# A softmax over rows: eight neighbouring rows per partition, taken from one block of 1024 rows or from 128 long stretches

## The chip, the cores and the metric

The kernel runs on one core of a Trainium2 chip, with the other cores idle. The metric is the device time of one execution in microseconds (us). The verdicts call 2% a difference. A profile is one execution; its span is about 2 us shorter than the time. HBM is the chip's main memory. KB and KiB both stand for 1024 bytes here, MB for a million.

A ratio below is the mean time of one kernel's fast runs over that of the kernel before in the same rounds, so it is not quite the ratio of the medians that stand beside it.

## The reference

The input has 32 x 512 = 16384 rows of 1024 float32 numbers, 67.1 MB, and the output is as large.

```python
def reference(x, temperature):            # temperature = 0.5
    scaled = x / temperature
    shifted = scaled - np.max(scaled, axis=-1, keepdims=True)
    exp_x = np.exp(shifted)
    return (exp_x / np.sum(exp_x, axis=-1, keepdims=True)).astype(np.float32)
```

Every row is computed by itself, so it doesn't matter which row sits in which partition, as long as it is stored where it came from.

## The kernel before

There are 16 tiles of 128 partitions with 8 rows each, in six buffers. The SyncE queue issues the loads, the ScalarE queue the stores. A tile goes through VectorE (maximum of each row, for four rows at a time), ScalarE (exponential and sum) and VectorE again (division in place), and is stored as a whole. When a tile's store has been issued, the load that will reuse its buffer is recorded; SyncE then waits until that store has landed.

```python
TILES = [[8]] * 16
BUFS = 6
# ...
    def dram(t, i):
        k = sum(TILES[i])
        block = t[P * first[i] : P * (first[i] + k), :]
        return block.rearrange("(p k) d -> p k d", p=P, k=k)
# ...
    def load():
        i = len(tiles)
        if i < len(TILES):
            xt = data.tile([P, sum(TILES[i]), d], f32, name="xt")
            nc.sync.dma_start(out=xt, in_=dram(xf, i))
            tiles.append(xt)
# ...
    def store(g):
        i, _, _, part = groups[g]
        if part:
            a, k = part
            nc.scalar.dma_start(out=dram(of, i)[:, a : a + k, :], in_=tiles[i][:, a : a + k, :])
            if a + k == sum(TILES[i]):
                load()
```

## Time and profile before

| | before |
|---|---|
| time, median of 3 runs | 318.23 us (318.12 to 318.53) |
| profiled span | 316.0 us |
| VectorE, ScalarE busy | 75%, 47% |
| data moved | 134.25 MB, 425 GB/s over the span |
| packets of 32 KB | 2048 loads, 2048 stores |

The transfers bound this kernel: the prediction below shows the lines and how they say so. The rate of the transfers in 40 equal slices of the span, from the page of the kernel before:

```profile
GB/s 332 411 452 423 373 460 415 452 425 431 436 427 440 427 444 423 444 419 448 415 452 411 452 408 456 423 444 427 436 431 432 440 423 444 419 444 419 452 411 274
```

One slice is 7.9 us. Neighbouring slices swing by some 30 GB/s presumably because packets of 32 KB are counted as wholes; averaged over two slices the rate is near 433. The dip to 373 in the fifth slice is where the first store begins. The last slice holds the end of the last store.

In the kernel before a 32 KB packet takes 1213 ns almost without exception: 53 of the 2048 load packets take more than 1240 ns, none of the 2048 store packets does. 49 of the 53 are in two places, the very first packets of the kernel and the moments before the first store.

### The profile page before, as it was taken

Reading aid. Unit: us, or ns where it says so; the run is one execution under the profiler, and the core shown is the slowest. Engines: PE = TensorE matmul, PEld = TensorE weight load, DVE = VectorE, ACT = ScalarE, POOL = GpSimd, SP = SyncE. Lnnn points to the kernel's source line nnn. Section 1 sums busy time; section 2 is a strip of 40 time slices with the busy share of each in tenths; the row PEclk is TensorE's granted clock in tenths of the full one; section 3 lists DMA queues with packets and bytes.
Section 4 is the critical chain, followed back from the end, with each engine's and each line's share of the span. In section 5 each row is a group of like instructions: output and inputs, shape, how many; then the busy total and the mean of one; then the engine's idle time right before and its main releaser. Section 6 shows DMA issues by size and latency. Waiting matters only on the chain.

```text
span 316.0 us, 620 instructions
## 1 busy us (share of the span) xinstructions
DVE 235.5 (75%) x224; ACT 149.6 (47%) x257; POOL 0.2 (0%) x4
## 2 busy tenths in 40 slices
DVE  0399999999689494994949859497693976949720
ACT  0176666666526255361554605546064560645500
POOL 0000000000000000000000000000000000000000
DMA  8999999999999999999999999999999999999996
GB/s 332 411 452 423 373 460 415 452 425 431 436 427 440 427 444 423 444 419 448 415 452 411 452 408 456 423 444 427 436 431 432 440 423 444 419 444 419 452 411 274
DMA packets 4612, 134.25 MB, mean 425 GB/s; under 512 B 512, under 2 KB 512, under 8 KB 512
## 3 DMA queue, kind: packets, MB, share of 16 engines
q1 hardware_dynamic: 2304, 67.11, 49.7%
q10 hardware_dynamic: 2304, 67.11, 49.2%
q14 instruction: 4, 0.03, 0.0%
HBM read 67.11 MB, written 67.11 MB: 425 GB/s over the span
## 4 chain that ended last, share of the span: by engine, by line
DVE 49%; DMA 32%; another core or an unknown queue 9%; ACT 5%; issue 1%; DVEq 0%; SPq 0%
DVE top L70 29%; DMA xt<-in_x_dram 20%; DVE xt L93 18%; DMA out_dram<-xt 12%; ACT xt L79 5%; DVE recip L91 1%; DVE bias L73 1%; DVEq L147 0%; SPq L61 0%
## 5 line engine op out<-in xcount | busy, mean ns | idle before, releaser
L79 ACT ACTIVATE xt<-xt,bias 128x1024 f32<-128x1024 f32 x128 | 145.4, 1137 | 136.8 <-DVE recip L91 119.4
L70 DVE TENSOR_REDUCE top<-xt 128x4 f32<-128x4096 f32 x32 | 141.3, 4416 | 62.6 <-DMA xt<-in_x_dram 62.6
L93 DVE TENSOR_SCALAR xt<-xt,recip 128x1024 f32<-128x1024 f32 x128 | 87.7, 749 | 1.1
L79 ACT ACTIVATION_READ_ACCUMULATOR xt<-xt,bias 128x1 f32 x128 | 23.9, 187 | 0.0
L79 ACT ACT_TABLE_LOAD x1 | 1.3, 1283 | 13.0 <-DMA xt<-in_x_dram 13.0
L91 DVE RECIPROCAL recip<-sums 128x4 f32<-128x4 f32 x32 | 5.5, 171 | 2.1 <-ACT xt L79 2.1
L73 DVE TENSOR_SCALAR bias<-top 128x4 f32<-128x4 f32 x32 | 5.4, 170 | 1.1
L133 POOL MEMSET const-bfloat16-1.0<- 128x1 bf16 x1 | 0.1, 101 | 0.0
L133 POOL MEMSET const-uint8-127<- 128x1 uint8 x1 | 0.1, 101 | 0.0
L133 POOL MEMSET const-float32-0.0<- 128x1 f32 x1 | 0.1, 98 | 0.2 <-issue 0.2
L133 POOL MEMSET const-float32-1.0<- 128x1 f32 x1 | 0.1, 98 | 0.0
## 6 DMA issues: line engine op xcount, KB each, us to landing
xt<-in_x_dram SPq DMA_DIRECT2D x16, 4096.0 KB, 50.2
out_dram<-xt ACTq DMA_DIRECT2D x16, 4096.0 KB, 38.6
```

The costliest lines, as they stand in the source:

```text
L70: nc.vector.tensor_reduce(out=top, in_=tiles[i][:, a : a + k, :], axis=mybir.AxisListType.X, op=extreme)
L73: nc.vector.tensor_scalar_mul(bias, in0=top, scalar1=-scale)
L79: nc.scalar.activation(tiles[i][:, a + b, :], tiles[i][:, a + b, :], mybir.ActivationFunctionType.Exp, bias=bias[:, b : b + 1], scale=scal ...
L91: nc.vector.reciprocal(recip, sums)
L93: nc.vector.tensor_scalar_mul(tiles[i][:, a + b, :], in0=tiles[i][:, a + b, :], scalar1=recip[:, b : b + 1])
L133: nc = _bacc.Bacc("TRN2", target_bir_lowering=False, num_devices=1)
```

## The change

The intent: let partition p own one long stretch, rows 128p to 128p+127, for the whole kernel, and let a tile take the next eight rows of every stretch. The tile's form in the core's memory and the run of one partition (8 rows, 32 KB) stay as they are. The distance in HBM between one partition's run and the next, called the pitch below, grows from 32 KB to 512 KiB.

```diff
     def dram(t, i):
-        k = sum(TILES[i])
-        block = t[P * first[i] : P * (first[i] + k), :]
-        return block.rearrange("(p k) d -> p k d", p=P, k=k)
+
+        rows = t.rearrange("(p r) d -> p r d", p=P)
+        return rows[:, first[i] : first[i] + sum(TILES[i]), :]
```

## The prediction

> **What bounds the kernel now.** I read the page of the profile from the top. Its first three parts nearly settle the matter, so I give them first.
>
> ```profile
> span 316.0 us, 620 instructions
> DVE 235.5 (75%) x224; ACT 149.6 (47%) x257; POOL 0.2 (0%) x4
> ...
> DMA  8999999999999999999999999999999999999996
> ...
> DMA packets 4612, 134.25 MB, mean 425 GB/s; under 512 B 512, under 2 KB 512, under 8 KB 512
> ...
> q1 hardware_dynamic: 2304, 67.11, 49.7%
> q10 hardware_dynamic: 2304, 67.11, 49.2%
> ```
>
> No compute engine is full: VectorE works 75% of the span, ScalarE 47%. The DMA row is 9 in all but the first and the last of 40 slices, and the two queues together fill 98.9% of the 16 DMA engines' span. So the kernel is bound by its transfers, from the first microsecond to nearly the last. Of the 2304 packets of a queue, 256 are under 512 B (16 transfers times 16 engines: the completion writes). The other 2048 are 16 tiles times 128 partitions: one packet is one partition's eight rows, 8 x 4 KB = 32 KB. Its mean duration is 0.497 x 16 x 316.0 / 2048 = 1.227 us on the load queue and 0.492 x 16 x 316.0 / 2048 = 1.215 us on the store queue. That is about 27 GB/s for one engine, 428 to 432 for sixteen.
>
> Next, the busy time by stretches, to see whether the rate depends on the mix of loads and stores (columns: stretch, its length, DVE, ACT, POOL, clock, DMA share, GB/s).
>
> ```profile
> 0.00:12.90 12.90, 0.00 (x0) 0.00 (x0) 0.20 (x4) 1.00 0.90 366
> ...
> 76.00:120.00 44.00, 35.40 (x34) 21.79 (x39) 0.00 (x0) 1.00 1.00 433
> 120.00:165.00 45.00, 31.80 (x32) 22.77 (x40) 0.00 (x0) 1.00 1.00 433
> ...
> 300.00:316.00 16.00, 2.35 (x4) 0.00 (x0) 0.00 (x0) 1.00 0.80 344
> ```
>
> The middle runs flat at 433 GB/s. A rate as flat as this in every stretch looks like the engines' own ceiling, not like memory that answers late now and then.
>
> Third, the waits and the chain that ended last, to see what the compute side hides.
>
> ```profile
> DVE top L70 <- DMA xt<-in_x_dram: 62.6, 12, 13.0
> ...
> 263.25 4.43 DVE top L70
> 267.71 0.17 DVE bias L73
> 267.88 0.09 DVE recip L91
> 267.99 2.74 DVE xt L93 x4
> 270.73 4.34 DVE top L70
> 275.17 0.18 DVE recip L91
> 275.38 2.74 DVE xt L93 x4
> 278.12 4.47 another core or an unknown queue
> 282.62 4.43 DVE top L70
> ```
>
> VectorE is idle for 62.6 us in all before the maximum of a new tile, always for a load. In the chain a tile comes every 282.62 - 263.25 = 19.37 us; VectorE works for about 14.9 us of it and waits 4.47 us. The page puts 49% of the chain on VectorE, but that is how it followed the releases. The period is that of the transfers: 8.39 MB (4.19 loaded, 4.19 stored) in 19.37 us is 433 GB/s, the very rate of the stretches.
>
> **What the Trainium skill says.** Three places bear on this, all on its page "DMA: Bandwidth & Descriptors".
>
> Section "Where 436 GB/s comes from" puts the ceiling of the 16 ports at 435.2 GB/s. The trace agrees: 433 in the steady part. Hence almost nothing can be gained by any layout: 435.2 / 433 is 0.5%.
>
> Section "Latency and other measured facts" has a row on HBM row pitch at large powers of two. It gives copies of tiles of 128 partitions x 16 KiB between HBM tensors, per direction: a pitch of 512 KiB between partitions gave 207 GB/s, 2 MiB 164, 4 MiB and 8 MiB 103, and 4 MiB padded by 4 KiB gave 214, called full. The page says that the cause (aliasing of HBM channels) is inferred, not verified. Twice 214 is 428, close to the 425 of this page; the trace of before shows nothing of a larger pitch.
>
> Section "The descriptor swizzle" says which partitions an engine serves: four neighbours and four more 32 further on. So at one moment sixteen engines work on partitions four apart. If they run in step, their addresses in HBM are 4 x 32 KB = 128 KiB apart now, and will be 4 x 512 KB = 2 MiB apart. The page of before doesn't list partitions by engine; no run here shows it.
>
> **The change part by part.** Nothing on an engine changes. Compared in the built programs, both kernels have the same rows in the same order on all engines: 130 on VectorE, 35 on ScalarE, 3 on SyncE. The SBUF side is the same too: 128 partitions with 32 KB each. What changes is only the address of each partition's 32 KB in HBM, for loads and stores alike. Before, tile i is one block of 4 MB, and partition p starts 32 KB after p-1. Afterwards partition p owns rows 128p to 128p+127, and tile i takes rows 8i to 8i+7 of each; partition p starts 128 x 4 KB = 512 KB after p-1.
>
> Added or removed instructions: 0. Softmax works row by row, so no result depends on which row sits in which partition. Packets: the run is 8 adjacent rows, still 32 KB contiguous, so still 2048 per direction and the same 134.2 MB. Issue: the pattern is partition, then one run, as before; the 32 transfers are issued long ahead of or under other transfers, and cost nothing now. Ends of the kernel: every transfer still uses all partitions, so the first load and the last store keep their form.
>
> What is left is the duration of a packet, and here I chose the skill's row for 512 KiB: it is exactly the new pitch, in both directions, as here. Estimate from it: 214 / 207 = 1.034 times the packet time of before.
> - Transfers in the span now: (0.497 + 0.492) x 316.0 = 312.5 us. The other 3.5 us are the first issue and the gaps at the end.
> - Afterwards, with the whole effect: 312.5 x 1.034 = 323.1 us, plus 3.5 = 326.6 us of span, plus the 318.23 - 316.0 = 2.2 us by which the time exceeds the profiled span: 328.8 us, 3.3% slower.
> - With no effect: 318.2.
>
> Nothing hides it. The transfers are the path throughout, and VectorE's wait of 4.47 us per tile grows by the same 19.37 x 0.034 = 0.66 us. I don't take the whole effect. The tiles here have runs of 32 KB where the row's have 16 KiB, so changes of run are half as frequent, and 207 against 214 is small enough that ramps could make part of it. About 70% of the added 10.6 us gives 7.3, hence 325.5 us.
>
> **The rivals.**
>
> One: the pitch does nothing at 512 KiB. For it: before already has a power of two between partitions (32 KB), and its rate is at the ports' ceiling without a dip. The two cores of a domain could together draw more than this one does (the skill's "HBM Reference", section "Specifications (TRN2)", gives 716 GB/s per domain; no run here shows it), so memory has room to spare, and only a loss larger than that room shows at all. The steps in the row from 4 MiB to 2 MiB (103 to 164, a factor 1.6) continued down two octaves would also lie far above the ceiling. Then the time is 317.5 to 319. This is the strongest rival, and with partial forms of it (up to 2%, 324.6 us) I give it 42%.
>
> Two: the aliasing is worse than in the row. Loads and stores use the same pitch, with tiles that lie only a few times 32 KB apart, and a packet of 32 KB keeps an engine in one place for twice as long. If two streams fall on the same channels as at the row's pitch of 2 MiB, the packets take 214 / 164 = 1.305 times as long: 312.5 x 1.305 + 5.7 = 413.5 us. Such a case would leave VectorE idle over half the time. Against it: the row measured this very pitch in both directions and found 3%. I give about 7% to anything above 338.
>
> Three: VectorE takes over. Its 235.5 us of work is 80 us short of the span and its instructions don't change, so it can't.
>
> Four: it becomes faster, because 128 separate streams spread better than one block. At the ceiling of 435.2 GB/s throughout, 134.25 MB take 308.5 us, plus 3.5 + 2.2 = 314.2 us, 1.3% faster. So 2% isn't within reach; 3% is left for what I haven't understood.
>
> **Range and chances.** The centre is 325.5 us. The low end, 317, is the first rival. The high end, 338, is about twice the effect of the skill's row (2 x 10.6 + 318.2 = 339). The line of 2% lies at 324.6, inside the spread of the size of the effect; the whole effect of the row is beyond it, and this tips it: slower 55%, same 42%, faster 3%.
>
> **What would show it right or wrong.** In the profile of the changed kernel the counts of packets (2304 per queue), the bytes and the number of instructions must be the same, and the durations of the instructions on VectorE and ScalarE too. If my step on the pitch is right, the GB/s row drops to about 420 in the middle, evenly from the first slices, where only loads run, to the last; the queues' shares stay near 49%, which over a longer span means packets of about 1.25 us; and VectorE's wait for loads grows from 62.6 us by the added time. If the rate stays at 433, the first rival is right. If only one queue's packets grow, reads and writes differ in how they take the pitch. If the rate falls in some stretches alone, the distance between the load's and the store's tiles matters and not the pitch by itself. My prediction is wrong if the time is under 317 or above 338, and its reason is wrong if the added time lies in gaps between transfers.

## The result, and the profile after

The changed kernel took 322.97 us in the median of six runs (320.39 to 324.86), against 318.13 (317.79 to 318.53) in six runs of the kernel before. The ratio is 1.0148, with a 95% interval of 1.0099 to 1.0196: slower by 1.5%. The runs spread over 4.5 us, where those of the kernel before spread over 0.7 us.

The page of the changed kernel, the lines that answer to those of before:

```profile
span 321.3 us, 620 instructions
...
DMA  8999999999999999999999999999999999999966
GB/s 322 428 424 445 375 420 441 420 426 432 432 436 432 420 436 428 412 420 445 428 428 445 432 425 441 428 416 432 424 436 433 416 449 412 436 432 396 449 290 265
DMA packets 4612, 134.25 MB, mean 418 GB/s; under 512 B 512, under 2 KB 512, under 8 KB 512
...
q1 hardware_dynamic: 2304, 67.11, 49.5%
q10 hardware_dynamic: 2304, 67.11, 48.4%
```

Instructions, packets and bytes are the same. The load queue (q1) fills 0.495 x 16 x 321.3 = 2545 us of engine time where it had 0.497 x 16 x 316.0 = 2513; the store queue (q10) has 2488 and had 2488. So only load packets became longer. The other thing to see is the end of the rows: before, only the last slice was below 9 at the end of the DMA row; now the last two are at 6, with 290 and 265 GB/s. Some of the 16 engines have nothing to do there while others still work.

Two stretches of the kernel before that the prediction doesn't show, and then those of the changed kernel (columns as in the prediction: stretch, length, DVE, ACT, POOL, clock, DMA share, GB/s):

```profile
12.90:30.00 17.10, 16.69 (x13) 10.63 (x18) 0.00 (x0) 1.00 0.99 429
30.00:76.00 46.00, 45.58 (x45) 29.45 (x51) 0.00 (x0) 1.00 1.01 427
```

```profile
12.90:30.00 17.10, 16.38 (x11) 10.45 (x17) 0.00 (x0) 1.00 1.00 431
30.00:76.00 46.00, 45.48 (x46) 29.14 (x51) 0.00 (x0) 1.00 1.00 419
...
120.00:165.00 45.00, 33.82 (x35) 22.13 (x39) 0.00 (x0) 1.00 1.00 428
...
240.00:280.00 40.00, 29.67 (x30) 18.78 (x33) 0.00 (x0) 1.00 1.01 430
...
300.00:321.30 21.30, 5.64 (x9) 4.60 (x8) 0.00 (x0) 1.00 0.73 315
```

While only loads run (12.9 to 30 us) the rate is 431, which the kernel before had too (429). Where the stores begin (30 to 76 us) it is 419 against 427. In the middle it is 428 to 432 where it was 433 to 434. So there is no even drop to 420, only one of about 1% in the middle, beside a lower rate where the stores begin and a longer end.

The waits and the chain of the changed kernel say where the end comes from:

```profile
DVE top L70 <- DMA xt<-in_x_dram: 67.6, 12, 13.3
...
247.70 4.43 DVE top L70
...
267.66 4.43 DVE top L70
...
282.53 5.30 another core or an unknown queue
287.85 4.43 DVE top L70
```

The last tile's maximum (L70) starts at 287.85 us; in the chain of the kernel before it starts at 282.62. From there to the end it takes 321.3 - 287.85 = 33.45 us, and it took 316.0 - 282.62 = 33.38. So all of the added 5.3 us has gathered before the last load landed. It gathered little by little: tiles come 19.96 us (267.66 - 247.70) and 20.19 us (287.85 - 267.66) apart, against 19.37 in the prediction's chain. VectorE's wait for loads grew by 67.6 - 62.6 = 5.0 us.

The packets' own durations refine this. In the changed kernel 175 load packets take over 1240 ns, against 53, and 25 store packets, against none. Summed, the packets of the load queue took (1240.4 - 1225.8) ns x 2048 / 16 engines = 1.9 us per engine more, those of the store queue 0.1 us. That is an average of 2.0 us, and the kernel lost 5.3. The difference is in how the 16 engines part. Each engine writes a completion mark when its share of a transfer is done: a queue has 256 packets of 4 bytes, 16 for each of 16 transfers. These marks show the last load's share done on the first and on the last of the 16 (us from the start of the span, as in the chain):

```
                     first engine done   last engine done   apart
before, last load        279.8 us            282.1 us       2.3 us
after,  last load        280.1 us            287.5 us       7.3 us
```

The first of these marks comes 0.3 us later than before, their mean 1.8 us (282.5 against 280.7), as the packets' durations say, and the last 5.4 us; the tile's maximum starts 0.4 to 0.5 us after the last mark on both sides. 5.2 us is what the chain lost. (The trace doesn't name the engine of a packet, so the first and the last need not be the same engines on both sides.) The distance grew through the whole kernel: 0.8 us at the third load, when no store had begun, 3.1 at the fifth, 4.7 at the tenth, 7.3 at the last.

### The profile page after: what moved, and what is told of

It is laid out like the page before. It is cut to its first block, busy times and chain, and to the rows that moved or that the text cites. A ratio compares the mean times of both kernels' runs of the same rounds, so it can differ in the third digit from the quotient of the medians.

```text
span 321.3 us, 620 instructions
## 1 busy us (share of the span) xinstructions
DVE 235.6 (73%) x224; ACT 149.6 (47%) x257; POOL 0.2 (0%) x4
## 4 chain that ended last, share of the span: by engine, by line
DVE 71%; another core or an unknown queue 17%; DMA 4%; ACT 3%; issue 1%; DVEq 0%
DVE top L70 42%; DVE xt L93 26%; DMA xt<-in_x_dram 4%; ACT xt L79 3%; DVE recip L91 1%; DVE bias L73 1%; DVEq L147 0%
## 5 line engine op out<-in xcount | busy, mean ns | idle before, releaser
L70 DVE TENSOR_REDUCE top<-xt 128x4 f32<-128x4096 f32 x32 | 141.3, 4416 | 67.7 <-DMA xt<-in_x_dram 67.6
```

The source lines that it names most:

```text
L70: nc.vector.tensor_reduce(out=top, in_=tiles[i][:, a : a + k, :], axis=mybir.AxisListType.X, op=extreme)
```

## The experiments

Twelve kernels were run, each on the chip beside the kernel before. "Slow load packets" means packets of 32 KB that took over 1240 ns, in the profiled run. Three of the kernels give wrong results, and are named so.

**Loads alone, stores alone.** The two kernels use the new layout on one side only, so the rows come out permuted (wrong; relative error 1.39 in both, correct bytes moved).

```diff
     def dram(t, i):
+        k = sum(TILES[i])
+        if t is xf:                       # load_long; "t is of" in store_long
+            rows = t.rearrange("(p r) d -> p r d", p=P)
+            return rows[:, first[i] : first[i] + k, :]
+        block = t[P * first[i] : P * (first[i] + k), :]
+        return block.rearrange("(p k) d -> p k d", p=P, k=k)
```

> Wrong on purpose: the loads use the 512 KiB pitch of the change, the stores the contiguous blocks of before, so rows come out permuted. Theory A (the added 4.8 us come from load packets that are slowed by the pitch of the loads themselves: 175 load packets over 1.24 us against 53, hardly any store packet): 322 to 324 us here, over 150 slow load packets. Rival B (it is the long pitch of the stores that slows the loads beside them): 317.5 to 319, about 50 slow packets. Rival C (both streams must have the pitch, so that reads and writes meet at the same places): 317.5 to 319.5 here and in store_long.

> Wrong on purpose: loads contiguous as before, stores with the 512 KiB pitch. Theory A: 317.5 to 319, about 50 slow load packets. Rival B: 322 to 324, over 150. Rival C: 317.5 to 319.5. If the two add up (part from each), about 320 in both.

The loads alone: 319.52 us (318.85 to 322.08), ratio 1.0058 (1.0034 to 1.0083); the profiled run is the slow one of 322.08, with 151 slow load packets and the last load's engines 6.1 us apart. The stores alone: 318.96 us (318.51 to 320.10), ratio 1.0037 (1.0023 to 1.0051), with 74 slow load packets and 2.7 us apart. The pages of the two, first the loads alone, then the stores alone:

```profile
span 320.2 us, 620 instructions
...
GB/s 315 434 430 434 389 422 442 422 436 434 430 434 430 434 418 422 450 430 430 426 434 438 423 438 422 438 430 430 430 426 439 422 430 430 426 442 405 446 299 266
```

```profile
span 316.9 us, 620 instructions
...
GB/s 331 414 447 438 389 430 443 418 453 410 451 410 451 418 443 430 430 434 426 455 405 459 401 456 418 447 426 434 434 426 448 414 451 410 451 418 443 430 401 256
```

The two weak slices at the end (299 and 266) come with the long pitch on the loads; with it on the stores the end is that of the kernel before. But the page of the loads alone is of its slowest run; the other five took 318.85 to 319.82 us, so that end needn't be typical of it. None of the three theories has all its numbers: theory C comes nearest in time (317.5 to 319.5 in both), but each half has a cost that is clear of the noise, and neither median comes near 322. Nor can the count of slow load packets show where the cost of the stores alone comes from: two kernels below that cost nothing have 64 and 72, and the mean load packet of the stores alone takes 1225.8 ns, as before.

**The change again, without an edit.** This was to settle whether the halves add up.

> The changed kernel once more, unedited. If the two halves simply add (loads alone 1.0058, stores alone 1.0037), 1.0095, that is 321.0 us. If the long pitch on both sides costs more than the sum, 1.013 to 1.017, 322 to 323.5 us. The spread of its runs should again be over 1.5 us where the kernel before has under 0.8; slow load packets over 130, and the last loads of the 16 engines should end over 5 us apart.

322.42 us (320.83 to 323.36), ratio 1.0136 (1.0114 to 1.0159). The spread of its runs is 2.5 us, there are 158 slow load packets, and the last load is done on the first engine at 279.4 us and on the last at 286.7, again 7.3 us apart. The halves add up to 1.0095; the whole is 1.0136. Both sides together cost more than the sum, but the interval of the sum (up to about 1.013, if both halves lie at their upper ends) overlaps that of the whole, so this is not shown.

**Is it the power of two?** Two kernels with right results: in one each partition has a stretch of 120 rows (480 KiB) for 15 tiles and the 16th tile is a contiguous block; in the other the tensor is cut into halves, with stretches of 64 rows (256 KiB).

```diff
+    LONG = 120                            # pitch480
     def dram(t, i):
+        k = sum(TILES[i])
+        if first[i] + k <= LONG:
+            rows = t[: P * LONG, :].rearrange("(p r) d -> p r d", p=P)
+            return rows[:, first[i] : first[i] + k, :]
+        block = t[P * first[i] : P * (first[i] + k), :]
+        return block.rearrange("(p k) d -> p k d", p=P, k=k)
```
```diff
+    LONG = 64                             # pitch256
     def dram(t, i):
+        k = sum(TILES[i])
+        start = first[i] // LONG * LONG
+        rows = t[P * start : P * (start + LONG), :].rearrange("(p r) d -> p r d", p=P)
+        return rows[:, first[i] - start : first[i] - start + k, :]
```

> Right results: each partition holds a stretch of 120 rows (pitch 480 KiB, no power of two), 15 tiles of it, and the last tile is a contiguous block. Theory P (aliasing at a power of two, as the Trainium skill's row on row pitch has it): 317.5 to 319, about 50 slow load packets. Rival S (spread: 128 places over the whole tensor are touched in each tile, whatever their distance): 321.5 to 324, about 160 slow packets.

> Right results: the tensor in two halves, each partition a stretch of 64 rows in each, pitch 256 KiB. Theory P: the effect shrinks with the pitch, 318 to 320.5. Rival S: half as wide a spread, still 320.5 to 323.

With 480 KiB: 318.11 us, ratio 1.0006 (0.9994 to 1.0018), 64 slow load packets, last load's engines 2.6 us apart. With 256 KiB: 317.83 us, ratio 1.0005 (0.9992 to 1.0018), 59 and 1.8 us. Both are the kernel before to within a thousandth. At 480 KiB a tile is spread over nearly the same width of HBM as at 512, so the spread isn't the cause (rival S fell). And at 256 KiB, a power of two, there is nothing either: that the pitch is a power of two is not enough.

**Four KB beside it.** A distance of 480 KiB might be harmless for being smaller than 512. So each partition gets a stretch of 127 rows (508 KiB), with tiles of 8 rows, one of 7, and a contiguous last one of 1 row per partition. The control has the same tiles at 512 KiB.

```diff
-TILES = [[8]] * 16
+TILES = [[8]] * 15 + [[7], [1]]           # long17 and pitch508
+    LONG = 127                            # pitch508, with dram() as in pitch480
```

> Control for the next run: the changed kernel at 512 KiB, with its last tile cut into one of 7 rows and one of 1 row. 320.5 to 325 us, over 120 slow load packets, by every theory.

> Same tiles as the control, but each partition's stretch is 127 rows, pitch 508 KiB, and the last tile (1 row) is a contiguous block. Theory P (a power of two): the 4 KiB are enough, 317.5 to 319.5 us and about 60 slow load packets. Rival D (any distance beyond some 480 KiB, power of two or not): as the control, 320.5 to 325.

The control: 321.57 us (320.45 to 322.69), ratio 1.0112 (1.0092 to 1.0133), 119 slow load packets. With 508 KiB: 318.19 us (318.11 to 318.34), ratio 1.0007 (0.9994 to 1.0020), 72 slow load packets. First the control's page, then that of 508 KiB:

```profile
span 318.7 us, 629 instructions
...
q1 hardware_dynamic: 2448, 67.11, 49.7%
q10 hardware_dynamic: 2448, 67.11, 48.8%
```

```profile
span 316.3 us, 629 instructions
...
q1 hardware_dynamic: 2448, 67.11, 49.7%
q10 hardware_dynamic: 2448, 67.11, 49.2%
```

The shares are nearly equal, but they are of different spans: 0.497 x 16 x 318.7 = 2534 us of load packets against 0.497 x 16 x 316.3 = 2515. A pitch smaller by less than 1% takes the whole loss away, so the exact value of 512 KiB matters and not its rough size. That this is because it is a power of two fits, but isn't shown: all the harmless pitches lie below 512 KiB, and none above it was run (516 KiB would tell a power of two from anything that begins at 512).

**When in the kernel?** The slow load packets of the changed kernel come in bursts. Sorted by the order in which the 16 engines take their 8 packets of a load, 93 of the 127 slow ones after the fourth load are at the fourth or fifth packet. In time, of 125 slow load packets between 45 and 275 us, 102 lie within 1.5 us of the moment when an engine finishes one store transfer, although only 584 of 1506 load packets there do. Not every such moment has a burst: the tenth and the eleventh load of this run have no slow packet at all. Two things meet at that moment: the stores go over to their next transfer, and the loads' own partitions jump (the Trainium skill, "DMA: Bandwidth & Descriptors", section "The descriptor swizzle", gives an engine four neighbouring partitions and four others 32 further on; the trace doesn't list partitions, so no run here shows it). Storing each tile in two halves was to part them.

```diff
-TILES = [[8]] * 16
+TILES = [[4, 4]] * 16                     # long_half (512 KiB), block_half (blocks)
```

> The changed layout, 512 KiB pitch, with each tile stored in two halves of 4 rows (32 store transfers of 16 KB runs in place of 16 of 32 KB; loads unchanged). In the changed kernel the slow load packets come in bursts, nearly all while the loads are at the fourth or fifth of an engine's 8 packets, which is when one store transfer ends and the next begins. Theory H (the hand-over from one store transfer to the next sets the bursts off): two bursts per load tile, slow load packets about twice as many (250 or more), and 1.5 times the loss or more: 2.0 to 3.0% over block_half. Rival J (the loads' own jump from the fourth to the fifth partition of an engine sets them off): one burst per load tile as before, the same loss of 1.0 to 1.7%.

> Control for long_half: the kernel before with stores in halves. By every theory 317 to 319.5 us, 50 to 80 slow load packets.

The control itself missed what every theory expected: 326.06 us (323.65 to 328.06), ratio 1.0249 (1.0193 to 1.0306; unclear at 2%). With the long pitch it was 326.91 us, ratio 1.0286 (1.0236 to 1.0335), with 235 slow load packets against 153 in the control. The intervals overlap, so the pitch's own part can't be read here; neither H's 2 to 3% over the control nor J's 1.0 to 1.7% came. What the page of the control shows:

```profile
span 323.3 us, 655 instructions
...
DVE  0399999999926499991694966929759999995000
...
DMA  8999999999999999999999999999999999999991
GB/s 324 450 401 436 405 416 444 428 450 418 442 409 434 432 458 401 438 422 430 434 420 423 450 414 428 424 454 411 426 440 397 441 411 426 431 432 428 434 403 49
```

VectorE is done three slices before the end, and the last slice moves only 49 GB/s: few engines are still busy. The completion marks have the 16 engines 7.7 us apart at the last store (1.8 in the kernel before), and up to 14.3 us in the middle. The loads also run ahead: the last one is done at 274.7 us (282.1 before), and from the ninth on each load begins 4 to 7 us after the packets of the one before it have ended (at most 1.4 us in the kernel before). So with stores in halves the engines drift apart even with contiguous blocks. Whether the unequal packets (loads of 32 KB beside stores of 16 KB) do it, or the earlier and more frequent stores, isn't shown.

One thing can be taken from the pair. In the kernel with the long pitch, 137 of the 164 slow load packets after the fourth load are at an engine's first or second packet of the load and only 5 at the fourth or fifth. So the loads' own jump between partitions (rival J) doesn't set the bursts off. But the hand-over of the stores doesn't by itself either (theory H). Of the slow load packets between 45 and 275 us, 151 of 169 are within 1.5 us of the end of a store transfer, which says little, as 1085 of all 1566 load packets there are. And in the fifth to the eighth load of this kernel, where the hand-overs fall at the fourth to seventh packet, 207 load packets are that near and none of them is slow. The bursts come from the ninth load on, where each load begins after a pause of 4 to 8 us: 132 of the 157 slow packets there are at the first or second packet of the load. What sets the bursts off stays open.

**Shorter runs.** The row on HBM row pitch in the Trainium skill ("DMA: Bandwidth & Descriptors", section "Latency and other measured facts") was taken with tiles of 128 partitions x 16 KiB. Tiles of 4 rows give that shape, with 32 tiles and 12 buffers. The row's copies go between HBM tensors, though, and those of this kernel between HBM and the core's memory.

```diff
-TILES = [[8]] * 16
-BUFS = 6
+TILES = [[4]] * 32                        # long4 (512 KiB), block4 (blocks)
+BUFS = 12
```

> Tiles of 4 rows at the 512 KiB pitch, 32 tiles, 12 buffers: runs of 16 KB for loads and stores, the very shape of the Trainium skill's row, which has 207 against 214 GB/s. If the size of my step was off because runs are twice as long here (it assumed changes of run cost), long4 takes 1.025 to 1.04 times as long as block4. If the length of the run doesn't matter, 1.01 to 1.017.

> Control for long4: contiguous blocks of 512 rows, 32 tiles, 12 buffers. 316 to 320 us by every theory: the same bytes, a little more overhead per transfer, a shorter fill and drain.

Long pitch: 319.33 us (319.12 to 320.06), ratio 1.0039 (1.0022 to 1.0056). Blocks: 319.20 us (319.14 to 319.30), ratio 1.0037 (1.0022 to 1.0052). There is no difference beyond the intervals, so both expectations for long4 missed: with tiles of 4 rows the pitch of 512 KiB costs nothing that can be seen here, although there are twice as many hand-overs. The edit changes the number of tiles and buffers with the run, so the length of the run is the likely reason and not the only one. (Both are 0.4% slower than the kernel before. A packet of 16 KB takes 611 ns, and two of them 9 ns more than one of 32 KB.)

**The distance between loads and stores.** Finally, does a read at one offset of the stretch collide with a write at another? The result of a tile is stored three tiles further on (wrong), so that at the hand-over both streams are at the same offset.

```diff
-        return rows[:, first[i] : first[i] + sum(TILES[i]), :]
+        at = first[i] if t is xf else first[(i + 3) % len(TILES)]
+        return rows[:, at : at + sum(TILES[i]), :]
```

> Wrong on purpose: the changed kernel, but the result of tile i is stored three tiles further on in each partition's stretch (round the end). When one store transfer hands over to the next, the loads are now in the tile at the same offset in their stretch, where in the changed kernel they lead by three or four tiles (96 to 128 KB). Theory R (a read and a write at a set distance in the stretch collide): the loss changes clearly, over 1.02 or under 1.008. Theory Q (only the 512 KiB pitch between the engines' addresses counts, not the distance between the two streams): as the changed kernel, 1.011 to 1.017, and over 130 slow load packets, three quarters of them near the end of a store transfer.

322.32 us (319.48 to 323.88), ratio 1.0118 (1.0077 to 1.0158), 157 slow load packets, of which between 45 and 275 us 75 of 103 lie within 1.5 us of a store transfer's end (724 of all 1506 load packets do). That is the changed kernel again: theory Q. The distance between the streams doesn't matter, or not enough to be seen.

The profiled runs with 16 tiles of 8 rows, by when the last load is done on the first and on the last engine (us from the start of the span); the added span follows the last engine:

| run | first engine done | last engine done | last, against before | span, against before |
|---|---|---|---|---|
| before | 279.8 us | 282.1 us | | 316.0 us |
| pitch256 | 280.3 | 282.1 | 0.0 | 0.0 |
| pitch480 | 280.2 | 282.8 | +0.7 | +0.7 |
| store_long | 280.3 | 283.1 | +0.9 | +0.9 |
| meet | 280.2 | 285.3 | +3.2 | +4.3 |
| load_long (its slowest run) | 280.3 | 286.4 | +4.3 | +4.2 |
| after_again | 279.4 | 286.7 | +4.6 | +4.6 |
| after | 280.1 | 287.5 | +5.4 | +5.3 |

The first engine is never late by more than 0.5 us. The pitch doesn't slow the transfers as a whole by as much as the kernel loses; it holds some engines back, and the tile waits for the last. (In meet the last store's engines, too, end further apart: 3.2 us, against 1.8 before.)

No experiment pointed to a version that clearly beats the kernel before. The best of all, 256 KiB, is within its noise, and 4096 packets of 1213 ns on 16 engines are 310.5 us of its 316.0.

## Why the prediction was right or wrong

The measured 322.97 us lies in the range of 317 to 338 and 2.5 us from the centre. The outcome that I thought likeliest (slower by over 2%, 55%) didn't come; the ratio of 1.0148 is on the side to which I gave 42%. That the time came so near the centre is partly luck: the sum was of an even loss on every packet, and what came is a smaller loss on the average engine and an unevenness between engines that no step had.

*The bound.* Right. The transfers set the time on both sides of the change, VectorE's wait grew by 5.0 us of the 5.3, and instructions, packets and bytes were unchanged.

*The pitch of 512 KiB costs transfer time.* Right in direction, and in keeping with the reason named: 480, 508 and 256 KiB cost nothing, 512 does (1.0136 and 1.0148). These runs show that this one pitch is harmful; that it is so as a power of two, and that HBM channels alias, is still inferred.

*The size.* This is the term that was mis-sized. "Estimate from it: 214 / 207 = 1.034 times the packet time of before" made 10.6 us of 312.5 us of transfers. Measured, the packets took 2.0 us longer on the average engine, the last engine was done 5.4 us later, and 5.3 us is what the span lost. One thing that the step passed over: the row's copies go from HBM to HBM, and no run here shows that loads into and stores from the core's memory must lose the same share. My 70% brought the estimate to 7.3 us, nearer, but for a wrong reason: "The tiles here have runs of 32 KB where the row's have 16 KiB, so changes of run are half as frequent" supposed that shorter runs lose more. The runs say the opposite: with tiles of 4 rows (16 KB) the pitch costs nothing (1.0039 against 1.0037), with tiles of 8 (32 KB) some 1.4%.

*Nothing hides it, and the loss is even.* The first half is right: what the last engine lost came through to the end. The second, "the GB/s row drops to about 420 in the middle, evenly from the first slices, where only loads run", is wrong. With only loads running there was hardly a loss (the first tile's maximum starts at 13.30 us against 12.96, then 431 GB/s, and no slow packet in the second and third load). In the changed kernel it came in bursts, most of them near the hand-overs of stores, and from the first to the last engine it differed by 5 us.

*The rivals.* The first, that the pitch does nothing at 512 KiB, is refuted by pitch508 against long17, which differ by 3.4 us with ranges that don't meet; at 256 KiB its forecast of no loss came true. The second, much worse aliasing through two streams a few runs apart, didn't occur, and meet shows that their distance hardly counts. The third and the fourth didn't occur. What no rival had was a loss that strikes single engines.

*The signs that I named.* "If only one queue's packets grow, reads and writes differ in how they take the pitch" is what the page showed, and it was half a trap: the load packets grew, but the long pitch on the stores alone also cost 0.37%, and the packets don't show where: its 74 slow load packets and 13 slow stores are much like the 64 and 12 of pitch480, which cost nothing.

*Slips in the working.* With the second rival's 413.5 us VectorE would be idle for 43% of the time (235.5 us of work), not over half. "So at one moment sixteen engines work on partitions four apart" is too simple by the section that it cites, where engine 7 begins at partition 28 and engine 8 at 64; four apart holds within each group of eight engines. And 70% of 10.6 us is 7.4, not 7.3. None of these changes the outcome.

## What to carry to other kernels

Look at the pitch from partition to partition in HBM as well as at the length of a run: 512 KiB cost this kernel 1.4%, and one row less, 508 KiB, nothing. A pitch above 512 KiB wasn't tried. When a kernel is bound by its transfers, ask when the last of the 16 engines is done, not only what rate they have together: weak slices just before the last one mean that some engines lag, and every tile waits for them. And be wary of storing in smaller pieces than were loaded: here that alone cost about 2.5% (1.9 to 3.1%), for a reason that stays open.

## What the Trainium skill lacked or had wrong

- "DMA: Bandwidth & Descriptors", section "Latency and other measured facts", the row on HBM row pitch: it has a pitch of 512 KiB at 207 against 214 GB/s, 3% down, for copies of tiles of 128 x 16 KiB between HBM tensors. It has no figure for loads into and stores from the core's memory: here tiles of that shape lost nothing (1.0039 against 1.0037), and tiles of 128 x 32 KiB lost 1.4%. Nor does it say that loads alone keep their rate (431 GB/s between 12.9 and 30 us).
- The same row's advice is to pad by 4 KiB. These runs tried 4 KiB less only, which the row doesn't have: 508 KiB gave 1.0007.
- That row calls its mechanism (channel aliasing) an inference, and no page says in what form such a loss comes: in bursts (102 of 125 slow load packets of the changed kernel within 1.5 us of the end of a store transfer, where 584 of all 1506 are), and unevenly over the engines (the first was done 0.3 us later, the last 5.4 us).
- No page has the cost of storing in smaller pieces than were loaded: loads of 32 KB beside stores of 16 KB, all from contiguous blocks, took 1.0249 times as long as equal ones of 32 KB, and equal ones of 16 KB only 1.0037. The page's section "Queues, rings and completion order" tells of turns by packets, but gives no figure for this.
